# A decoder layer on one core: tile 5's search is held back in the recording until the search of tiles 7 and 6 is over

## The chip, the core and the metric

The kernel runs as one program on 1 core of a Trainium2 chip. The core has five engines with a queue of instructions each: TensorE (PE in the profile, with PEld for its weight loads), VectorE (DVE), ScalarE (ACT), GpSimd (POOL) and SyncE (SP, which issues the DMAs). Each queue is worked off in its order; an instruction that waits for another engine holds up all that stands behind it on its own engine. The metric is device time in microseconds for one execution of the whole layer.

## The reference, cut to what matters

The layer takes 1024 tokens of width 1024 and computes a mixer and a SwiGLU feed-forward part, each with a residual and a layer norm. The part around the change is the sparse attention of the mixer:

```python
logits = jnp.einsum('bqhd,bsd->bqhs', iqb, ik_f) * (IDX_DIM ** -0.5)      # 8 index heads
score = jnp.einsum('bqh,bqhs->bqs', w, jax.nn.relu(logits))
score = jnp.where(causal[None], score, -jnp.inf)
_, idx = lax.top_k(score, k_sel)                                          # 256 keys for each query
...
s = jnp.einsum('bqhd,bqkhd->bhqk', qb, kg) * (HEAD_DIM ** -0.5)
p = jax.nn.softmax(jnp.where(valid[:, None], s, -jnp.inf), axis=-1)       # 8 attention heads
o = jnp.einsum('bhqk,bqkhd->bqhd', p, vg)
```

Every query may look at the 256 keys with the highest score among those before it. Beside the attention the mixer has four groups of causal pooling on 512 channels (u), whose result goes through a small product (w_pool) into the output projection.

## The kernel before, in words

The 1024 queries are cut into 8 tiles of 128, on the partitions. Tile i sees 128(i+1) keys. Tiles 0 and 1 see at most 256 keys and need no selection; tiles 2 to 7 do. The stages that matter here come in this order:

1. **Score loop** (lines 788 to 818). For tiles 2 to 7, and for each of 8 index heads: TensorE makes `lg`, ScalarE its relu, VectorE adds it, weighted, onto `score_X` (8 VectorE instructions for each tile). GpSimd then writes the causal limit into the tile's last 128 columns.
2. **Projections** (to line 982). TensorE makes u, k and v (`pj` and `pair`). For each of the four pooling groups, VectorE's `ub_V<-ub_V` (u_split, line 856) is followed by ScalarE's copy `phi_V`, GpSimd's remainder `plo_V` and TensorE's `po`; GpSimd also makes the remainders of the weights (`ws_W`, w_split, line 906) for k and v. For each of 8 tiles of k, ScalarE and VectorE write the transposed keys (`kr_K`).
3. **Attention** (from line 982), in units of one head pair and one tile: four head pairs with tiles 7 and 6 in turn, then four with 5 and 4, then 3 and 2, then 1 and 0. A unit is: TensorE's `s`, VectorE's masking and maximum (an instruction that the profile calls CUSTOM_DVE_ANT_0, `sm_H<-s,score_X`, 128x1024 for tile 7, 128x768 for tile 5), ScalarE's exponential, GpSimd's normalization, TensorE's transposes `pT`, their copies by ScalarE and VectorE, and TensorE's product `o`.
4. Output projection, norm and feed-forward part, to the end.

The selection itself (`bisect`, line 642) is a binary search for the 256th value, in 31 steps on 16-bit halves of the score. One VectorE step is a comparison over all keys of a tile with an accumulated count (`junk_X<-keys...`) and two instructions on one number per query (`colsD_X` or `colsE_X`). After the last step come the masks: seven instructions that turn `score_X` into a mask of 0 and a large negative number. Four such searches exist. Tiles 4 and 3 share one and tile 2 has its own, both on ScalarE (`TILES_A`, columns `colsA_X`). Tiles 7 and 6 share one on VectorE (`colsD_X`, `keysD_T`), and tile 5 has its own on VectorE (`colsE_X`, `keys_T`, 128x768).

What sets the order. A search is a Python generator, called a stream here, which stops before each step and names the engine and the step's cost. While the other instructions are recorded, `fill` (line 768) is asked before each of them: it lets every stream advance whose next step fits, by the kernel's own table of costs, before that instruction's operands are ready. While the letters V, A and G are in `pinned` (from `open_stream`, line 745, to `pinned.clear()`, line 982) each instruction of VectorE, ScalarE and GpSimd is also marked to stay in the order in which it was recorded (line 175). Instructions recorded with the pins off carry no such mark: the framework's own scheduler places them on their engine among the others, as early as their data and its own estimate allow. A mask that isn't there yet when attention wants it is fetched by `need(i)` (line 764), called from `u_exp` (line 1041), which is after line 982, with the pins off: it advances tile i's stream until its mask is recorded.

Of the kernel before, what the change touches and what calls it, by code (L numbers as in the profile page):

```python
# [41 lines left out]
NORM = 2  # L42
NORM_SMALL = 2
STEP_ORDER = "SPNT"
COPY_N = 4
COPY_V = (0,)
START_A = 5
# [3 lines left out]
SLACK = {"V": 0.3, "A": 0.4}  # L51
# [130 lines left out]
def decoder_layer_kernel(  # L182
# [560 lines left out]
    streams = []  # L743
# [7 lines left out]
    def start(st):  # L751
        return max(st[0], queues[st[1][0]].t)

    def advance(st):
        fill, times.fill = times.fill, None
        q = queues[st[1][0]]
        try:
            st[1] = next(st[2])
        except StopIteration:
            streams.remove(st)  # L760
        st[0] = q.t
        times.fill = fill
# [4 lines left out]

    def fill(q, until):
        while True:
            todo = [st for st in streams if st[1][0] == q.name and start(st) + st[1][1] <= until + SLACK.get(q.name, 0.0)]  # L770
            if not todo:
                return
            advance(min(todo, key=lambda st: (start(st), -max(st[3]))))
# [293 lines left out]
    def u_trans(u):  # L1067
        g, pr, i = u
        for e, (sm, st) in enumerate(live.pop(u)[0]):
            for j0 in range(0, i + 1, 4):  # L1070
# [7 lines left out]
                n_cp[0] += 1  # L1078
                if n_cp[0] % COPY_N in COPY_V:
                    V.tensor_copy(dst, pv)  # L1080
# [53 lines left out]
    for n_, u in enumerate(units):  # L1134
        g, pr, i = u
        for step in STEP_ORDER:
            if step == "S":
# [398 lines left out]
    first = {}  # L1536
# [366 lines left out]
```

## Time and profile before

| | |
|---|---|
| median of 3 runs | 1336.13 us (1334.67 to 1336.29) |
| the profiled execution's own time | 1334.65 us |
| its span, first to last instruction | 1332.9 us |
| PE busy | 1201.6 us (90% of the span) |
| DVE busy | 1081.6 us (81%) |
| ACT busy | 640.0 us (48%) |
| POOL busy | 737.4 us (55%) |
| mean granted TensorE clock | 0.949 of full speed |

The shares are means over stages with different limits. In the strip of 40 slices of the page (33.3 us each, counted from 1) DVE reads 8 or 9 from slice 2 to slice 13, while PE falls to 6 in slices 11 and 12 and PEclk to 6 and 7 in slices 12 and 13: that is the end of the projections and the first part of attention. From slice 14 on the strip is led by PE.

### The profile page before, as it was taken

How to read it: one execution, taken by the hardware profiler on the slowest of the kernel's cores; microseconds unless marked ns; L12 is line 12 of the kernel's file. 1: busy time of each engine (PE TensorE's matmuls, PEld its weight loads, DVE VectorE, ACT ScalarE, POOL GpSimd, SP SyncE). 2: the span in 40 equal slices, each digit the busy share in tenths (PEclk: the TensorE clock that was granted, in tenths of full speed). 3: DMA queues.
4: the chain of work that ended last, by engine and by line, in shares of the span. 5: the costliest groups of instructions: out<-in, count | busy, mean ns of one | idle time of the engine just before them, and what ended most of it. 6: DMA issues, size and time to landing. Idle time of an engine off the chain costs nothing.

```text
span 1332.9 us, 16110 instructions
## 1 busy us (share of the span) xinstructions
PE 1201.6 (90%) x5462; PEld 936.7 (70%) x5462; DVE 1081.6 (81%) x1828; ACT 640.0 (48%) x1335; POOL 737.4 (55%) x509
## 2 busy tenths in 40 slices
PE   7979997888667997999789999999999999999996
PEld 6646575667434664788677878878787887878775
DVE  6898999999989788566687787777768787777698
ACT  3345785658756676535644343333333343333431
POOL 1392494565012354527678484755748485666848
PEclk8999998889867898999799999999999999999998
DMA  9540020302000066420030101112120101113113
GB/s 350 216 161 19 16 95 17 110 32 79 25 0 9 26 210 240 157 103 1 24 111 30 66 32 64 45 50 76 36 79 32 64 32 64 63 41 118 41 59 122
DMA packets 34904, 103.91 MB, mean 78 GB/s; under 512 B 3843, under 2 KB 3843, under 8 KB 33286
## 3 DMA queue, kind: packets, MB, share of 16 engines
q1 hardware_dynamic: 34822, 102.88, 21.6%
q8 instruction: 43, 0.70, 0.2%
q14 instruction: 39, 0.32, 0.1%
HBM read 93.42 MB, written 9.45 MB: 77 GB/s over the span
## 4 chain that ended last, share of the span: by engine, by line
PE 38%; DVE 6%; POOL 4%; issue 2%; ACT 1%; DVEq 0%; POOLq 0%; ACTq 0%
PE gu L169 24%; PE dn L169 14%; DVE act_W L169 2%; POOL wraw_R L169 1%; DVE utmp_X L169 1%; POOL wraw_W L169 1%; DVE gtmp_V L169 1%; POOL wblk_T L169 0%; DVE wblk_T L169 0%; DVE hr_H L169 0%; POOL hr_H L169 0%; DVE res_X L169 0%; DVE stat_C L169 0%; POOL wblk_V L169 0%; DVE wblk_V L169 0%
## 5 line engine op out<-in xcount | busy, mean ns | idle before, releaser
L169 PE MATMUL gu<-hr_H,wblk_T 128*128 128x512 f32 (+1 forms) x924 | 217.0, 387 | 2.9 <-POOL wblk_T L169 1.9
L169 PE MATMUL gu<-hr_H,wblk_V 128*128 128x512 f32 (+1 forms) x924 | 215.1, 384 | 3.7 <-POOL wblk_V L169 2.0
L169 PEld LDWEIGHTS gu<-hr_H,wblk_T 128*128 128x128 f32 x924 | 172.1, 191 | 39.0 <-POOL wblk_T L169 3.6
L169 PEld LDWEIGHTS gu<-hr_H,wblk_V 128*128 128x128 f32 x924 | 170.1, 188 | 40.1 <-POOL wblk_V L169 3.7
L169 DVE TENSOR_TENSOR res_X<-res_X,dn 128x512 f32<-128x512 f32 (+1 forms) x253 | 159.0, 678 | 15.2 <-PE dn L169 15.0
L169 POOL TENSOR_SCALAR sm_H<-sm_H,stat_X 128x1024 f32<-128x1024 f32 (+7 forms) x64 | 58.2, 922 | 152.7 <-DVE stat_X L169 109.9
L169 PE MATMUL pj<-ws_W,hT_H 128*128 128x512 f32 x456 | 120.2, 411 | 6.4 <-ACT pout_K L169 2.7
L169 POOL TENSOR_TENSOR wraw_R<-wraw_R 128x512 f32<-128x512 f32 x64 | 94.3, 1480 | 47.0 <-DVE wblk_T L169 23.7
L169 POOL TENSOR_TENSOR wraw_W<-wraw_W 128x512 f32<-128x512 f32 x60 | 86.6, 1450 | 58.0 <-DVE wblk_V L169 29.3
L169 PEld LDWEIGHTS pj<-ws_W,hT_H 128*128 128x128 f32 x456 | 85.9, 194 | 32.7 <-issue 11.5
L169 PE MATMUL dn<-wblk_T,act_W 128*128 128x512 f32 x324 | 79.8, 395 | 4.4 <-DVE act_W L169 4.4
L169 PE MATMUL dn<-wblk_V,act_W 128*128 128x512 f32 x324 | 78.5, 391 | 2.9 <-DVE act_W L169 2.5
L169 DVE TENSOR_SCALAR_CACHE_REDUCE junk_X<-keysD_T,colsD_X 128x1024 int16<-128x1024 int16 (+1 forms) x64 | 79.0, 1270 | 0.9
L169 PEld LDWEIGHTS dn<-wblk_T,act_W 128*128 128x128 f32 x324 | 61.0, 190 | 19.2 <-DVE act_W L169 6.5
L169 ACT ACTIVATE wblk_V<-wraw_R 128x512 fp32r<-128x512 f32 x56 | 35.3, 630 | 80.6 <-POOL wraw_R L169 62.2
L169 POOL TENSOR_TENSOR ws_W<-raw_R,ws_W 128x1024 fp32r<-128x1024 f32 x17 | 44.4, 2629 | 51.7 <-ACT ws_W L169 51.7
L169 PEld LDWEIGHTS dn<-wblk_V,act_W 128*128 128x128 f32 x324 | 60.4, 188 | 17.4 <-DVE act_W L169 4.2
L169 ACT ACTIVATE wblk_V<-wraw_W 128x512 fp32r<-128x512 f32 x53 | 33.1, 628 | 75.0 <-POOL wraw_W L169 56.4
L169 ACT ACTIVATE wblk_T<-wraw_W 128x512 fp32r<-128x512 f32 x56 | 35.0, 628 | 66.3 <-POOL wraw_W L169 50.2
L169 ACT ACTIVATE sm_H<-sm_H,stat_X 128x1024 f32<-128x1024 f32 (+7 forms) x64 | 49.0, 767 | 32.3 <-DVE stat_X L169 31.9
L169 ACT ACTIVATE wblk_T<-wraw_R 128x512 fp32r<-128x512 f32 x52 | 32.5, 627 | 60.9 <-POOL wraw_R L169 45.5
L169 PE MATMUL pT<-const_C,sm_H 128*128 128x128 f32 x288 | 48.3, 303 | 10.9 <-DVE qab_W L169 5.3
(305 smaller groups left out, 2812.2 us busy)
## 6 DMA issues: line engine op xcount, KB each, us to landing
wm_K<-in_wma_dram SPq DMA_DIRECT2D x16, 512.0 KB, 9.3
modraw_V<-in_wmc_dram SPq DMA_DIRECT2D x16, 512.0 KB, 4.5
wraw_R<-in_wg_dram SPq DMA_DIRECT2D x6, 1024.0 KB, 4.7
wraw_R<-in_wd_dram SPq DMA_DIRECT2D x12, 512.0 KB, 3.4
wraw_W<-in_wup_dram SPq DMA_DIRECT2D x12, 512.0 KB, 3.5
modraw_V<-in_wmg_dram SPq DMA_DIRECT2D x10, 512.0 KB, 4.3
wraw_R<-in_wup_dram SPq DMA_DIRECT2D x10, 512.0 KB, 3.5
wraw_W<-in_wg_dram SPq DMA_DIRECT2D x5, 1024.0 KB, 4.8
```

The lines of the kernel that those rows point to most:

```text
L169: ins_ = f(*a, **k)
```

## The change

`fill` no longer lets tile 5's stream advance as long as the stream of tiles 7 and 6 is open:

```diff
+LATE = [5]
...
     def fill(q, until):
         while True:
-            todo = [st for st in streams if st[1][0] == q.name and start(st) + st[1][1] <= until + SLACK.get(q.name, 0.0)]
+
+            first = [st for st in streams if 7 in st[3]]
+            todo = [st for st in streams if not (first and st[3] == LATE) and st[1][0] == q.name and start(st) + st[1][1] <= until + SLACK.get(q.name, 0.0)]
             if not todo:
                 return
             advance(min(todo, key=lambda st: (start(st), -max(st[3]))))
```

No instruction is added or taken away: each engine has the same instructions with the same operands. The stream of tiles 7 and 6 is still open when line 982 takes the pins off. So all of tile 5's steps and masks are now recorded without a mark, and the built program has them in other places on VectorE. The orders of GpSimd and SyncE are the same in both programs, and TensorE's is the same up to the attention of tiles 7 and 6. On ScalarE the steps of the two searches of tiles 4, 3 and 2 move a little.

VectorE at the end of the score loop, from the first score instruction of tile 7 (128x1024) to the first count of tiles 7 and 6 (`colsD_X<-score_X`). Before:

```order
L169 TENSOR_SCALAR score_X_77<-relu_K_563,const_C_78 128x1024
L169 SCALAR_TENSOR_TENSOR score_X_77<-relu_K_563,const_C_78,score_X_77 128x1024 x7
L169 TENSOR_SCALAR junk_X_607,colsD_X_615<-score_X_77 128x1024
L169 TENSOR_SCALAR junk_X_608,colsD_X_615<-score_X_77 128x896
L169 TENSOR_SCALAR colsD_X_615<-colsD_X_615 128x2 x3
```

The same place now, its last rows:

```order
L170 SCALAR_TENSOR_TENSOR score_X_77<-relu_K_563,const_C_78,score_X_77 128x1024
L170 SCALAR_TENSOR_TENSOR colsE_X_616<-colsE_X_616 128x1
L170 TENSOR_SCALAR junk_X_609,colsE_X_616<-keys_T_612,colsE_X_616 128x768
L170 SCALAR_TENSOR_TENSOR score_X_77<-relu_K_563,const_C_78,score_X_77 128x1024
L170 TENSOR_SCALAR colsE_X_616<-colsE_X_616 128x1
L170 SCALAR_TENSOR_TENSOR score_X_77<-relu_K_563,const_C_78,score_X_77 128x1024
L170 SCALAR_TENSOR_TENSOR colsE_X_616<-colsE_X_616 128x1
L170 TENSOR_SCALAR junk_X_609,colsE_X_616<-keys_T_612,colsE_X_616 128x768
L170 TENSOR_SCALAR junk_X_607,colsD_X_615<-score_X_77 128x1024
```

Tile 5's first count, its keys and five comparisons of its search now stand among the scores of tiles 6 and 7; before, none of them did.

VectorE around the third of the four pooling instructions `ub_V<-ub_V`. Before, with one step of tile 5 ahead of it (the third of 32 comparisons with `keys_T`):

```order
L169 SCALAR_TENSOR_TENSOR colsD_X_615<-colsD_X_615 128x2
L169 TENSOR_SCALAR junk_X_609,colsE_X_616<-keys_T_612,colsE_X_616 128x768
L169 TENSOR_SCALAR colsE_X_616<-colsE_X_616 128x1
L169 SCALAR_TENSOR_TENSOR colsE_X_616<-colsE_X_616 128x1
L169 SCALAR_TENSOR_TENSOR ub_V_1221<-ub_V_1221,ub_V_1222 128x1024
L169 TENSOR_SCALAR junk_X_607,colsD_X_615<-keysD_T_610,colsD_X_615 128x1024
```

The same place now, with the end of tile 5's search and its masks ahead of it:

```order
L170 TENSOR_SCALAR keys_T_612<-score_X_77,colsE_X_616 128x768
L170 TENSOR_SCALAR junk_X_609,colsE_X_616<-score_X_77,colsE_X_616 128x768
L170 TENSOR_SCALAR colsE_X_616<-colsE_X_616 128x1
L170 SCALAR_TENSOR_TENSOR score_X_77<-keys_T_612,colsE_X_616 128x768
L170 TENSOR_SCALAR score_X_77<-score_X_77 128x768
L170 TENSOR_TENSOR keys_T_612<-keys_T_612,score_X_77 128x768
L170 TENSOR_TENSOR junk_X_609<-junk_X_609,keys_T_612 128x768
L170 TENSOR_SCALAR score_X_77<-junk_X_609 128x768
L170 SCALAR_TENSOR_TENSOR ub_V_1221<-ub_V_1221,ub_V_1222 128x1024
L170 TENSOR_SCALAR junk_X_607,colsD_X_615<-keysD_T_610,colsD_X_615 128x1024
```

All 32 comparisons and all masks of tile 5 stand ahead of this instruction now, where 3 comparisons stood; ahead of the first `ub_V` it is 17 instead of 1, ahead of the second 29 instead of 2. Ahead of the first masking instruction of attention it is 32 instead of 20. From the first masking instruction of tile 5 on (128x768) the two orders hold the same work again.

## Rows read from the trace of the kernel before

**Rows 1.** Busy us by stretch: PE, PEld, DVE, ACT, POOL; then clock, DMA share, GB/s.
```profile
172.10:209.00 36.90, 33.75 (x148) 27.27 (x146) 36.06 (x62) 22.22 (x67) 27.70 (x19) 1.00 0.24 86
209.00:259.00 50.00, 39.05 (x135) 30.31 (x136) 48.85 (x78) 32.96 (x85) 28.34 (x16) 0.80 0.18 64
354.60:376.10 21.50, 2.61 (x7) 1.59 (x8) 20.11 (x49) 5.80 (x12) 0.00 (x0) 0.54 0.05 17
376.10:440.10 64.00, 50.76 (x224) 31.39 (x222) 56.25 (x135) 44.39 (x116) 16.35 (x14) 0.75 0.02 5
440.10:480.00 39.90, 37.06 (x251) 24.82 (x250) 32.13 (x75) 26.48 (x58) 14.55 (x14) 0.96 0.29 97
```

**Rows 2.** Waits of PE from 172 to 376 us: total us, times, longest.
```profile
PE s L169 <- DVE qab_H L169: 18.8, 1, 18.8
...
PE kT L169 <- DVE kr_K L169: 2.4, 1, 2.4
...
PE pj L169 <- DVE kr_K L169: 1.3, 1, 1.3
```

**Rows 3.** Busy DVE us of tile 5's `colsE_X` instructions by stretch; last row: all.
```profile
172.10:209.00 36.90, 2.72 (x10) 1.00 0.24 86
209.00:259.00 50.00, 2.83 (x9) 0.80 0.18 64
376.10:440.10 64.00, 21.36 (x58) 0.75 0.02 5
120.00:441.00 321.00, 52.74 (x145) 0.87 0.12 40
```

**Rows 4.** Timeline of DVE: start, us; two comparisons of tile 5 in a row.
```profile
361.75 1.07 DVE L169 TENSOR_SCALAR_CACHE_REDUCE junk_X<-keys_T,colsE_X 128x768 int16<-128x768 int16 x1
...
363.25 1.07 DVE L169 TENSOR_SCALAR_CACHE_REDUCE junk_X<-keys_T,colsE_X 128x768 int16<-128x768 int16 x1
```

**Rows 5.** Waits of DVE from 143.6 to 173 us.
```profile
DVE score_X L169 <- ACT relu_K L169: 1.8, 3, 0.8
DVE junk_X L169 <- POOL score_X L169: 1.5, 1, 1.5
```

**Rows 6.** Instructions on `colsE_X` and, for 209 to 250 us, `colsD_X`: ns min/median/max.
```profile
L169 DVE TENSOR_SCALAR colsE_X<-colsE_X x37: 132/153/155, 189.7 to 429.8; 128x1 f32<-128x1 f32 x35, 128x1 int16<-128x1 f32 x1, 128x1 int32<-128x1 int32 x1
L169 DVE SCALAR_TENSOR_TENSOR colsE_X<-colsE_X x31: 139/159/1214, 208.9 to 426.9; 128x1 f32<-128x1 f32 x31
...
L169 DVE SCALAR_TENSOR_TENSOR colsD_X<-colsD_X x6: 162/1808/2277, 213.8 to 243.7; 128x2 f32<-128x2 f32 x6
```

**Rows 7.** Timeline of DVE: third pooling instruction, and attention's first ones; tile 5's first.
```profile
238.81 1.23 DVE L169 SCALAR_TENSOR_TENSOR ub_V<-ub_V,ub_V 128x1024 f32<-128x1024 f32 x1
...
374.11 1.40 DVE L169 TENSOR_TENSOR qab_H<-qT,qab_H 64x512 fp32r<-64x512 f32 x2
376.10 1.22 DVE L169 CUSTOM_DVE_ANT_0 sm_H<-s,score_X 128x1024 f32<-128x1024 f32 x1 [0.58 <-PE s L169]
...
440.10 0.95 DVE L169 CUSTOM_DVE_ANT_0 sm_H<-s,score_X 128x768 f32<-128x768 f32 x1
```

**Rows 8.** Timeline of ACT and POOL behind the third pooling instruction.
```profile
240.06 1.06 ACT L169 ACTIVATE phi_V<-ub_V 128x1024 fp32r<-128x1024 f32 x1 [6.65 <-DVE ub_V L169]
...
241.20 2.39 POOL L169 TENSOR_TENSOR plo_V<-ub_V,phi_V 128x1024 fp32r<-128x1024 f32 x1 [3.71 <-DMA raw_R<-in_wv_dram]
243.56 4.69 POOL L169 TENSOR_TENSOR ws_W<-raw_R,ws_W 128x1024 fp32r<-128x1024 f32 x2
```

**Rows 9.** Timeline of PE: a product on those weights, then the last work before attention.
```profile
245.95 7.15 PE L169 MATMUL pair<-ws_W,hT_H 128*128 128x512 f32 x23 [2.56 <-POOL ws_W L169]
...
352.11 1.03 PE L169 MATMUL qT<-const_C,raw_R 128*128 128x128 f32 x8
354.64 1.35 PE L169 MATMUL s<-kr_K,qab_H 128*128 128x512 f32 x4 [1.49 <-ACT qab_H L169]
```

**Rows 10.** Timeline of ACT in attention: one comparison of tile 4's search.
```profile
388.39 0.81 ACT L169 ACTIVATE junkA_T<-keys_T,colsA_X 128x640 bf16<-128x640 uint16 x1
```

## The prediction, written before the changed kernel ran

> **What bounds the kernel now.** I read the busy time by stretch first, then tile 5's share of it, then who waits. From the end of the score loop (172.1 us) to the first masking instruction of tile 5 (440.1) VectorE is the busiest engine: 36.06 of 36.90 us, 48.85 of 50.00, and 20.11 of the 21.50 before attention begins, in which TensorE does 2.61 [rows 1]. TensorE's longest wait there is one of 18.8 us for VectorE's `qab_H` [rows 2]: it had the projections and the transposed queries of tile 7 ready at 352 us [rows 9], and attention's first masking instruction came at 376.1 [rows 7]. In the next 64.0 us VectorE is busy 56.25 us, 21.36 of them with tile 5's search [rows 1, 3]. So VectorE's queue sets the pace up to 440.1, TensorE's after it (37.06 of 39.90 us [rows 1]). What stands where in that queue is what the change alters.
>
> **What the change does.** By its words it holds tile 5 back. The order of the built program shows the opposite. Its steps are recorded after the pins are off, and the scheduler has put them ahead of work that they used to follow. All 32 comparisons and the masks stand before the third `ub_V`, where 3 comparisons stood, and before attention's first masking instruction, where 20 stood. No work is saved (52.74 us of tile 5 on VectorE in both [rows 3]). So three things count: the work that is pushed back, the wait that is filled, and what attention gains when tile 5 is out of its way.
>
> **1. VectorE reaches attention later.** Two comparisons of tile 5 in a row start 1.50 us apart [rows 4]. Twelve more of them stand ahead of attention now: 18.0 us. Its masks come too. What is left of the 21.36 us [rows 3] after twelve comparisons at the busy 1.07 of [rows 4] and their two small instructions at 0.15 and 0.16 (medians of [rows 6]), 16.6 us, is 4.8 us, to which I add 1.8 for the gaps and the few instructions between search and masks: 6.6. Together +24.6 us. Against it, in the score loop VectorE waited 1.8 us for ScalarE and 1.5 for GpSimd [rows 5], and tile 5's steps stand there now: -3.3.
>
> The third part is GpSimd. In a step, the instruction with two inputs on `colsE_X` has a median of 159 ns and a longest of 1214, while the one with a single input never took over 155; and between 209 and 250 us, where GpSimd works much, the same two-input instruction of tiles 7 and 6 has a median of 1808 [rows 6]. In the 21.50 us before attention GpSimd did nothing [rows 1], and a part of tile 5's search stood there; now it stands beside its work on `ws_W` and the pooling groups. Lower bound 0 (GpSimd has no more instructions than before, and each delays one VectorE instruction at most once). Upper bound: 24 steps move into that stretch (29 comparisons ahead of the second `ub_V`, less five in the score loop), each at 1.21 - 0.16 = 1.05: 25 us. I take +3, near the lower end, because in the trace the median of `colsE_X` is the short one although GpSimd worked beside its first steps. The Trainium skill, SBUF — State Buffer (Who interferes with whom), says that GpSimd and VectorE share a pair of ports as an exclusive lock and that a VectorE instruction with two SBUF inputs is held up whole by a reading GpSimd instruction. The trace agrees (159 ns against 1808). By it alone every moved step could be hit, and the sum would be the upper bound.
>
> VectorE: 24.6 - 3.3 + 3 = +24.3, so it is ready for attention at 376.1 + 24.3 = 400.4.
>
> **2. TensorE is late next.** The pooling chain runs through four queues in order: `ub_V` on VectorE, then `phi_V` on ScalarE (240.06, after a wait of 6.65 for it), `plo_V` on GpSimd, and behind `plo_V` in GpSimd's queue the weights `ws_W`, without which TensorE can't go on [rows 8, 9]. At the third `ub_V` (238.81 [rows 7]) tile 5 had used 2.72 + 2.83 = 5.55 us [rows 3] and will have used all 52.74: 47.2 us busy, or 51.3 at 1.50 us for each 1.38 busy. Less the 3.3 recovered, plus 3 for GpSimd: +51.0. TensorE resumes `pair` at 296.9 instead of 245.95. From there to the transposes of the queries (352.11 [rows 9]) its way is the same, without the waits of 2.4 and 1.3 us for `kr_K` [rows 2], since VectorE has less between those now; I add 1 us for the clock after the longer wait (it was 0.80 of full speed from 209 to 259 us, with waits [rows 1]). 352.1 + 51.0 - 3.7 + 1 = 400.4. From the transposes to the first masking instruction it takes 2.5 us to the first `s` [rows 9] and 2.0 from `qab_H` to the mask [rows 7]: 404.9. So TensorE takes over from VectorE as what is late, by 4 us, and attention starts **+28.8 us**. The 18.8 us that TensorE waited there are not gained. They turn into waits at `po` and `ws_W` earlier.
>
> Bounds: +21.3 (VectorE alone, GpSimd at its lower bound) and +50.8 (GpSimd at its upper bound, 22 us over the 3 taken).
>
> **3. The first half of attention gets shorter.** From the first mask of tile 7 to that of tile 5 (64.0 us) VectorE has 56.25 - 21.36 = 34.9 us left. ScalarE has 44.39, less three comparisons of tiles 4 and 3 that the order now has before attention, 3 x 0.81 [rows 10]: 42.0. TensorE has 50.76 at a clock of 0.75 [rows 1], 38.1 at full speed, and it comes to this stretch from work and not from a wait of 18.8 us. Three engines have about as much to do; none can fill the stretch. In the next one, led by TensorE, 37.06 x 0.96 = 35.6 us at full speed took 39.90, a share of 0.89. ScalarE's 42.0 at that share is 47.2. I take 47 us, so **-17**. Bounds: 42.0 (-22) with ScalarE never waiting, and 56 (-8) if TensorE starts cold again.
>
> From 440.1 on both programs have the same order on VectorE, so what is late there stays late: I see no work in it that could start before its units, and TensorE, which leads in the next stretch, waits there for the same units as before. I cost it at nothing.
>
> **Sum.** +28.8 - 17 = +11.8 us. The profiled execution took 1334.65 us, so 1346.5; the median of the runs is 1.5 us above it, which makes **1348 us**.
>
> **The rivals.** *A, not slower: VectorE alone counts.* If TensorE isn't late, attention starts at +21.3, and if ScalarE's work closes up to 42.0 us the stretch gives back 22.0: -0.7, or 1335 us. It decides wherever the stretch gets under 64.0 - 28.8 = 35 us with my start, or under 43 with VectorE's. For it speaks that VectorE was the busiest engine nearly throughout and that its work is the same. Against it: pooling and weights hang on `ub_V` one after the other, and TensorE is in front of attention by 18.8 us only, where it loses 51.
>
> *B, much slower: the start of attention costs more.* Place: the steps beside GpSimd, at about half the upper bound (+12 instead of +3), and a first half of attention of 52 us. Price: +37.8 - 12 = +26, or 1362 us. For it speaks the 1808 ns of tiles 7 and 6; against it the 155 ns limit of the single-input instruction, so that only one in three instructions of a step can be hit.
>
> *C, it does what it says:* tile 5's steps run after the masks of tiles 7 and 6. Then attention starts when TensorE is ready, at 352.1 + 4.5 = 356.6 or 19.5 us earlier, and all of tile 5, 52.74 us busy, stands beside the next stretch: 34.9 + 52.74 = 87.6 us instead of 64.0, +23.6. The sum is +4, or 1340 us. The order rules it out, as far as one engine's queue runs in its order.
>
> **Chances.** My forecast (+5 to +19) 0.60, A 0.15, B 0.22, C 0.03. A change of under 0.2% (2.7 us) can't be told from none with this kernel. A lies mostly within that, and partly below, and so a little of my forecast's lower side falls within it too: faster 0.08, same 0.11, slower 0.81. The range takes in A's upper half and B: 1336 to 1362 us; my forecast's own is 1341 to 1355.
>
> **What would show it.** In the changed kernel's trace: instructions on `colsE_X` from about 145 us and none after about 290; the third `ub_V` at about 290; TensorE idle for over 20 us before the first `po` and again before the second; no long wait for `qab_H`; the first mask of tile 7 at about 405 and of tile 5 at about 452. It is wrong in step 1 if VectorE passes the third `ub_V` far from 290, in step 2 if TensorE is found waiting for VectorE once more at `qab_H`, in step 3 if the stretch between the first masks of tiles 7 and 5 isn't 42 to 52 us, and altogether if that of tile 5 comes before 440.

## The result and the profile after

The changed kernel takes 1345.0 us (median of 3 runs, 1343.72 to 1346.84) against 1336.13: a ratio of 1.0071 with a 95% interval of 1.0048 to 1.0094. It is slower, by 8.9 us, and 1348 had been forecast. The profiled execution took 1345.0 us with a span of 1343.2, 10.3 more than the span before.

I cut both profiles at 172 us (the end of the score loop before; in the changed kernel the first count of tiles 7 and 6 comes at 176.86) and at three events of the program: the first masking instruction of tile 7, that of tile 5 and that of tile 3. First busy us by stretch of the kernel before; columns as in [rows 1].

```profile
110.00:172.00 62.00, 57.52 (x259) 38.05 (x258) 53.24 (x65) 42.75 (x71) 24.66 (x18) 1.00 0.04 14
172.00:376.10 204.10, 160.62 (x655) 127.16 (x655) 198.10 (x366) 134.21 (x366) 101.31 (x65) 0.88 0.17 58
376.10:440.10 64.00, 50.76 (x224) 31.39 (x222) 56.25 (x135) 44.39 (x116) 16.35 (x14) 0.75 0.02 5
440.10:490.81 50.71, 47.18 (x319) 31.91 (x318) 40.98 (x96) 35.89 (x78) 19.60 (x18) 0.97 0.37 122
```

The same of the changed kernel:

```profile
110.00:172.00 62.00, 57.03 (x256) 37.41 (x255) 57.23 (x83) 42.14 (x69) 22.22 (x16) 1.00 0.04 15
172.00:395.56 223.56, 164.78 (x659) 129.43 (x658) 211.44 (x410) 135.23 (x377) 100.85 (x65) 0.85 0.16 53
395.56:450.50 54.94, 48.17 (x216) 29.00 (x215) 36.43 (x72) 42.05 (x105) 15.50 (x14) 0.76 0.02 6
450.50:499.84 49.34, 47.10 (x329) 31.71 (x327) 40.71 (x96) 37.36 (x81) 19.77 (x18) 1.00 0.38 127
```

Attention starts 19.5 us later, its first half (mask of tile 7 to mask of tile 5) is 9.1 us shorter, and the rest is nearly the same: it is 10.4 us late at tile 5, 9.0 at tile 3 and 10.3 at the end. The third number behind the comma is VectorE's busy time; length less busy is called its waiting here, the short gaps between instructions included. Up to tile 3's first mask VectorE is busy 348.6 us before and 345.8 after, so it has no more to do; it waits 32.2 us before and 44.0 after. Of these 11.8 us more, 10.8 lie in the first half of attention (7.8 to 18.5) and 6.1 ahead of it; 4.0 were won up to 172 us and 1.1 behind the first half. Most of what is new ahead of attention are waits at the keys:

```profile
DVE kr_K L170 <- ACT kr_K L170: 5.2, 5, 1.8
```

VectorE's timeline, in answer to [rows 7]:

```profile
275.23 1.22 DVE L170 SCALAR_TENSOR_TENSOR ub_V<-ub_V,ub_V 128x1024 f32<-128x1024 f32 x1
...
393.57 1.41 DVE L170 TENSOR_TENSOR qab_H<-qT,qab_H 64x512 fp32r<-64x512 f32 x2 [1.24 <-ACT qab_H L170]
395.56 1.23 DVE L170 CUSTOM_DVE_ANT_0 sm_H<-s,score_X 128x1024 f32<-128x1024 f32 x1 [0.58 <-PE s L170]
...
436.30 1.23 DVE L170 CUSTOM_DVE_ANT_0 sm_H<-s,score_X 128x1024 f32<-128x1024 f32 x1 [3.91 <-PE s L170]
...
445.89 1.09 DVE L170 CUSTOM_DVE_ANT_0 sm_H<-s,score_X 128x896 f32<-128x896 f32 x1 [5.12 <-PE s L170]
```

TensorE's waits from 172 to 410 us, in answer to [rows 2] (total us, times, longest), and then its timeline ahead of attention, in answer to [rows 9]:

```profile
PE pair L170 <- POOL ws_W L170: 16.5, 4, 5.0
PE po L170 <- ACT ub_V L170: 14.9, 1, 14.9
PE po L170 <- ACT phi_V L170: 11.3, 1, 11.3
PE pair L170 <- ACT ws_W L170: 7.3, 1, 7.3
...
PE s L170 <- ACT qab_H L170: 1.7, 1, 1.7
```

```profile
390.21 1.03 PE L170 MATMUL qT<-const_C,raw_R 128*128 128x128 f32 x8
392.97 3.28 PE L170 MATMUL s<-kr_K,qab_H 128*128 128x512 f32 x8 [1.73 <-ACT qab_H L170]
```

The wait of 18.8 us for `qab_H` is gone; those on the pooling chain (`po` and `ws_W`) have grown from 16.8 to 52.0 us. TensorE reaches the transposes of the queries 38.1 us later, and now VectorE waits for what comes from it: at the keys and at `qab_H` behind ScalarE's part, and twice for long inside the first half.

### The profile page after: what moved, and what is told of

Same layout as the page of the kernel before. It is cut to its first block, busy times and chain, and to the rows that moved or that the text cites. A ratio compares the mean times of both kernels' runs of the same rounds, so it can differ in the third digit from the quotient of the medians.

```text
span 1343.2 us, 16107 instructions
## 1 busy us (share of the span) xinstructions
PE 1200.3 (89%) x5462; PEld 933.6 (70%) x5462; DVE 1077.9 (80%) x1828; ACT 639.9 (48%) x1335; POOL 734.5 (55%) x509
## 4 chain that ended last, share of the span: by engine, by line
PE 37%; DVE 6%; POOL 4%; issue 2%; ACT 1%; DVEq 0%; POOLq 0%; ACTq 0%
PE gu L170 23%; PE dn L170 14%; DVE act_W L170 2%; POOL wraw_R L170 1%; DVE utmp_X L170 1%; POOL wraw_W L170 1%; DVE gtmp_V L170 1%; POOL wblk_T L170 0%; DVE wblk_T L170 0%; DVE hr_H L170 0%; POOL hr_H L170 0%; DVE res_X L170 0%; DVE stat_C L170 0%; POOL wblk_V L170 0%; DVE wblk_V L170 0%
## 5 line engine op out<-in xcount | busy, mean ns | idle before, releaser
L170 PE MATMUL pj<-ws_W,hT_H 128*128 128x512 f32 x456 | 117.5, 404 | 3.9 <-DVE const_C L170 1.7
L170 PEld LDWEIGHTS pj<-ws_W,hT_H 128*128 128x128 f32 x456 | 83.8, 190 | 29.4 <-issue 10.1
L170 PE MATMUL pair<-ws_W,hT_H 128*128 128x512 f32 x144 | 44.1, 468 | 19.3 <-POOL ws_W L170 12.0
## 6 DMA issues: line engine op xcount, KB each, us to landing
wm_K<-in_wma_dram SPq DMA_DIRECT2D x16, 512.0 KB, 10.1
```

The source lines that it names most:

```text
L170: ins_ = f(*a, **k)
```

## The experiments

All times are medians; each ratio is to runs of the kernel before on the same chip. "Mask 7", "5" and "3" are the starts of the first masking instructions of these tiles in the profiled execution, busy and waiting are VectorE's from 110 us to mask 3, as above. From mask 3 to the end each program takes 842 to 847 us, so most of what a change does is settled there. The profiled execution lies up to 4.4 us off its kernel's median (e5: 1331.8 against 1327.3), so positions and medians agree no better than that.

| run | us | ratio to before, 95% | mask 7 | mask 5 | mask 3 | busy | waiting |
|---|---|---|---|---|---|---|---|
| before | 1336.13 | | 376.1 | 440.1 | 490.8 | 348.6 | 32.2 |
| changed | 1345.0 | 1.0071 [1.0048, 1.0094] | 395.6 | 450.5 | 499.8 | 345.8 | 44.0 |
| e1_held | 1339.6 | 1.0016 [1.0003, 1.0030] | 355.3 | 452.9 | 497.1 | 347.4 | 39.7 |
| e2_half | 1349.5 | 1.0102 [1.0087, 1.0117] | 372.1 | 459.1 | 503.8 | 345.8 | 48.0 |
| e3_chain | 1346.6 | 1.0085 [1.0070, 1.0101] | 409.1 | 459.4 | 505.2 | 354.5 | 40.8 |
| e4_warm | 1341.1 | 1.0040 [1.0025, 1.0055] | 395.1 | 448.0 | 497.3 | 345.1 | 42.2 |
| e5_split20 | 1327.3 | 0.9931 [0.9912, 0.9950] | 372.9 | 437.1 | 482.7 | 340.7 | 32.0 |
| e6_split10 | 1328.5 | 0.9944 [0.9928, 0.9959] | 362.9 | 442.6 | 483.5 | 342.8 | 30.6 |
| e7_split20_warm | 1326.4 | 0.9926 [0.9909, 0.9942] | 372.3 | 435.7 | 480.7 | 341.3 | 29.4 |
| e8_chain_off | 1336.7 | 1.0004 [0.9994, 1.0013] | 395.9 | 444.3 | 489.7 | 337.7 | 42.0 |
| e9_cols_split | 1332.8 | 0.9964 [0.9950, 0.9977] | 380.3 | 436.4 | 485.7 | 327.9 | 47.8 |
| e10_cols_split_before | 1318.8 | 0.9863 [0.9846, 0.9880] | 355.2 | 430.5 | 472.8 | 329.0 | 33.8 |
| e11_best | 1313.8 | 0.9825 [0.9808, 0.9841] | 359.9 | 423.9 | 467.4 | 320.9 | 36.5 |

**e1: tile 5 really held back.** In `advance`, VectorE is pinned while a step of tile 5 is recorded:

```
+        own = st[3] == LATE and "V" not in pinned
+        if own:
+            pinned.add("V")
         ...
+        if own:
+            pinned.discard("V")
```

> The changed kernel, with VectorE's queue kept in written order also while tile 5's steps are recorded in attention, so that none of its 32 comparisons can be moved ahead: by the order all 32 stand behind attention's first masking instruction. Theory 1 (the loss of 9 us comes from work of tile 5 that stands ahead of the pooling chain and of attention): the third ub_V is back near 235 us, attention starts when TensorE is ready, first mask of tile 7 at 354 to 360 us, no 18.8 us wait for qab_H; the first mask of tile 5 at about 445 because VectorE has 35 + 53 = 88 us of work up to it; in all 1336 to 1344 us, faster than the changed kernel. Theory 2 (holding tile 5 back costs by itself, wherever its steps land): 1345 us or more.

Most of the loss is gone, attention starts at 355.3 us and the third `ub_V` is at 236.3. So what cost the changed kernel its time is the work that was moved ahead, as theory 1 says. But nothing is gained over before either: tile 5's block now ends in front of its first unit, and TensorE stands still for it. Tile 5's first mask came at 452.9 us, where 445 had been expected: VectorE's work of 88.96 us fills most of the first half (its row, then TensorE's timeline at the end of it):

```profile
355.32:452.91 97.59, 62.12 (x322) 40.77 (x322) 88.96 (x242) 51.70 (x122) 17.04 (x16) 0.75 0.02 6
```

```profile
453.93 2.50 PE L170 MATMUL s<-kr_K,qab_W 128*128 128x512 f32 x6 [21.48 <-DVE stat_X L170]
```

**e2: 20 comparisons ahead, 12 and the masks in written order.** As e1, with `own` true only from the 24th step on.

> The changed kernel, but only the first 20 comparisons of tile 5 may be moved ahead; the other 12 and the masks are kept in written order in attention. Ahead of attention stand then as many comparisons as before the change (20), but 17 more of them than before ahead of the third ub_V. So VectorE's amount is that of before and only the pooling chain is late. Theory 1 (chain and amount count separately, the chain by about 1.25 us for each comparison): third ub_V at about 260 us instead of 238.8, TensorE at the queries' transposes at about 374 instead of 352, its wait for qab_H under 3 us, first mask of tile 7 at 376 to 380; total within 4 us of before, 1333 to 1340. Theory 2 (TensorE's lateness is what costs, VectorE's amount doesn't): most of the loss remains, 1342 us or more.

A miss. The third `ub_V` came at 252.6 us, `qab_H` was waited for 1.7 us, and attention started at 372.1, earlier than before, all as theory 1 has it or better; but the median is the highest of all (its interval overlaps those of e3 and of the changed kernel). TensorE's longest wait from 372 us on is of 14.1 us, for VectorE at tile 5's first unit:

```profile
PE s L171 <- DVE stat_X L171: 18.6, 8, 14.1
```

The order has all 12 comparisons and the masks between the 16th and the 17th masking instruction, so VectorE waited 20 us earlier in that half and then made TensorE wait. Theory 2's number came true, by another mechanism; e5 takes that mechanism away.

**e3: the same amount ahead, behind the pooling chain.** The planner's filling leaves tile 5 out; its steps start behind the fourth `ub_V`, three at each projection group:

```
+        for _ in range(PACE * (n_ > 9)):
+            for st in streams:
+                if st[3] == LATE:
+                    advance(st)
```

> The changed kernel with none of tile 5's steps ahead of the fourth ub_V; from there on its steps are recorded in order, three at each projection group, so that all 32 comparisons and the masks stand ahead of attention as in the changed kernel, but the pooling chain is not delayed. Theory 1 (VectorE's amount ahead of attention costs by itself): third ub_V near 235 us, TensorE waits again, at the projections and over 15 us at qab_H, first mask of tile 7 at 395 to 402 us, total 1342 to 1352. Theory 2 (only the late chain costs): first mask of tile 7 before 382 us, and with a first half of attention of 55 us a total of 1320 to 1332.

The third `ub_V` was early (233.9 us) and the loss stayed; the work ahead of attention costs by itself, since VectorE is busy for 226.7 of the 237.1 us from 172 to the first mask. TensorE waits not at `qab_H`, as expected (1.5 us), but at the keys that VectorE writes late:

```profile
PE kT L171 <- DVE kr_K L171: 37.7, 3, 29.6
PE pj L171 <- DVE kr_K L171: 17.9, 2, 10.5
```

Mask 7 came later than theory 1 said (409.1 for 395 to 402): VectorE's busy time is 8.6 us more than in the changed kernel, and this is the only order in which it lies above that of before.

**e4: TensorE busy in its short wait.**

```
+            warm = psA("warm")
+            for _ in range(FILLER):
+                tc.keep_in_program_order(T.transpose(warm[:, 0:P], ident, ident))
```

> The changed kernel with 14 transposes of the identity (nobody reads them) behind the transposes of the queries, so that TensorE has work in its wait of 1.73 us for qab_H. In the changed kernel the granted clock is 1.00 up to 390 us and 0.50 from 395.5 to 410, and VectorE waits 14 us for s up to tile 5's first mask. Theory 1 (the slow clock behind that short wait is the reason why the first half of attention took 54.9 us and not 47): the clock stays at 1.00, the stretch between the first masks of tiles 7 and 5 becomes 48 to 52 us, total 3 to 7 us less. Theory 2 (the clock falls because of the waits between the s units, or TensorE isn't what sets the pace there): the stretch stays at 54 to 56 us and the total within 1.5 us of the changed kernel's.

The changed kernel from 390 to 405 us, then the run with the transposes:

```profile
390.00:395.00 5.00, 3.27 (x16) 2.01 (x14) 3.67 (x6) 4.90 (x10) 0.00 (x0) 0.92 0.31 105
395.00:400.00 5.00, 3.85 (x9) 2.00 (x8) 4.38 (x7) 4.95 (x9) 0.00 (x0) 0.50 0.01 2
400.00:405.00 5.00, 5.00 (x10) 2.00 (x8) 2.58 (x6) 5.00 (x15) 1.95 (x2) 0.50 0.00 0
```

```profile
390.00:395.00 5.00, 4.81 (x30) 3.35 (x28) 3.70 (x7) 4.90 (x10) 0.00 (x0) 1.00 0.32 105
395.00:400.00 5.00, 3.22 (x9) 1.40 (x8) 4.77 (x8) 4.95 (x10) 0.00 (x0) 0.73 0.01 2
400.00:405.00 5.00, 5.00 (x10) 2.43 (x10) 2.41 (x5) 5.00 (x15) 2.21 (x2) 0.50 0.00 0
```

The granted clock held out a few us longer and then fell to its lower level (0.50, which is 1.2 GHz) all the same. The first half took 52.9 us instead of 54.9, between the two theories. The total is 3.9 us less; all four runs lie below the three of the changed kernel (1340.6 to 1342.3 against 1343.7 to 1346.8), but the intervals of the two ratios still touch, so some gain is likely and its size is not shown.

**e5 and e6: how much goes ahead.** The first steps of tile 5 are recorded ahead of the queries' split and are free to move; the next step is pinned behind it; the rest is free again and spreads over the first half (e5 `HOIST = 23`, 20 comparisons; e6 `HOIST = 13`, 10).

```
+    need(7)
+    need(6)
+    st5 = next(st for st in streams if st[3] == LATE)
+    for k_ in range(HOIST):
+        advance(st5)
     for i in (7, 6):
         q_make(i, qr[i], qp[i])
+    pinned.add("V")
+    advance(st5)
+    pinned.discard("V")
```

> The changed kernel, with the first 20 comparisons of tile 5 free to move ahead (they stand ahead of the second ub_V, as in the run with 20 before it) and one step behind them tied to the queries' split of attention, so that the other 12 comparisons and the masks can't pass it but are spread freely over the first half of attention, as before the change. Ahead of attention VectorE has what it had before the change; only the pooling chain is late. Theory 1 (the run with 20 was slow only because its 12 comparisons and masks stood in written order in one block ahead of tile 5's first unit, with TensorE waiting 14 us for it; the late chain costs nothing as long as TensorE reaches the queries before VectorE): first mask of tile 7 at 371 to 374 us, first mask of tile 5 at 434 to 441, total 1331 to 1338. Theory 2 (the late chain itself costs): 1342 or more.

> As the run before, with 10 comparisons of tile 5 free to move ahead instead of 20, and 22 and the masks spread over the first half of attention. Theory 1 (what counts is how long VectorE waits in all up to about 490 us, since its busy time there is the same in every order): ahead of attention it waits less, as the chain is hardly late (third ub_V at 240 to 245), first mask of tile 7 at 358 to 362; in the first half it has 71 us of work and waits under 10, so the first mask of tile 5 comes at 432 to 441 and the total is 1328 to 1338. Theory 2 (comparisons in attention stand in the way of TensorE's units, as in the run that held all of them back): 1339 or more.

Both are faster than before, by 0.7 and 0.6%. Theory 2 fails in both; theory 1 has e6's total right and its range for e5 was too high. But its reason, that VectorE's busy time is the same in every order, doesn't hold: of the 8.2 and 7.4 us that the two are ahead of before at mask 3, 7.9 and 5.8 lie in the busy time (348.6 to 340.7 and 342.8) and the rest in waiting. Why these orders keep VectorE busy for less, no run separates. In e5 the third `ub_V` is at 253.7 us, 14.8 later than before, and TensorE reaches the queries at 368.1; that lateness costs nothing, since it takes only from the 18.8 us that TensorE used to wait. Its stretches up to mask 5:

```profile
172.00:372.92 200.92, 159.95 (x662) 126.61 (x660) 190.35 (x351) 135.24 (x376) 100.97 (x65) 0.90 0.18 59
372.92:437.08 64.16, 54.54 (x236) 32.71 (x238) 58.73 (x146) 46.26 (x113) 16.73 (x14) 0.76 0.03 9
```

Against the changed kernel: the last 12 comparisons and the masks go back into the first half of attention, which grows by 9.2 us, while its start comes 22.6 us earlier. VectorE waits 5.4 us in that half instead of 18.5.

**e7: e5 with idle transposes**, 14 as in e4 and 5 behind the scores of each of the first four units.

> The run with 20 comparisons ahead and 12 spread, with transposes of the identity that nobody reads: 14 behind the queries' transposes and 5 behind the scores of each of attention's first four units. Theory 1 (gaps of about half a microsecond between the first units are what keeps the granted clock at 0.50 for the first 15 us): clock over 0.8 in the 15 us from the first s on, total 3 to 6 us under the run without them. Theory 2 (VectorE sets the pace in that stretch, since it has 56 us of work in 64): within 2 us of the run without them.

Theory 2: within 1 us of e5, and the clock was at 0.50 from 380 to 390 us in both.

**e8: the pooling chain off VectorE.** `u_split` does on GpSimd what wrote `ub_V` on VectorE; the planner's account is kept as it was.

```
-        V.scalar_tensor_tensor(cur[:, 16:PADW], cur[:, 16:PADW], 1.0 / WINDOWS[g], own[:, 16:PADW], ALU.mult, ALU.subtract)
+        G.tensor_scalar(cur[:, 16:PADW], cur[:, 16:PADW], 1.0 / WINDOWS[g], None, ALU.mult)
+        G.tensor_tensor(cur[:, 16:PADW], cur[:, 16:PADW], own[:, 16:PADW], ALU.subtract)
```

> The changed kernel, with the pooling difference that writes ub_V taken from VectorE to GpSimd, as a scaling and a subtraction (no other work is changed, and tile 5's 32 comparisons still stand ahead of the projections' end). The pooling chain no longer passes VectorE's queue. Theory 1 (VectorE's queue is what makes TensorE late at po and ws_W): the waits of 14.9 and 11.3 us at po are gone, TensorE reaches the queries' transposes before 365 us and waits over 10 us for qab_H; attention starts when VectorE is ready, 380 to 390 us; total 1331 to 1341. Theory 2 (GpSimd becomes the late one, with 4 x 3.5 us more in its queue ahead of ws_W): TensorE waits for ws_W over 25 us in all, total 1343 or more.

The waits at `po` are down to about 2 us each, as expected, and the total lies in theory 1's range, but not on its way: TensorE then waits at the next thing from VectorE's queue, and attention starts where it did.

```profile
325.54 1.09 PE L170 MATMUL kT<-const_C,rope_V 128*128 128x128 f32 x4 [43.55 <-DVE kr_K L170]
```

Of the 10.1 us won on the changed kernel up to mask 3, 8.1 lie in VectorE's busy time, and 4.9 of these are the four `ub_V` that GpSimd took over. Why the first half is 48.3 us there, with the clock at 0.86 in place of 0.76, no run separates; what differs is named under step 3 below.

**e9 and e10: the form of the small instructions**, in the changed kernel and in the one before.

```
-                V.tensor_scalar(pr, cntc, 0.0, float(1 << b), ALU.is_ge, ALU.mult)
+                for m in range(nt):
+                    V.tensor_scalar(one(pr, m), one(cntc, m), 0.0, float(1 << b), ALU.is_ge, ALU.mult)
...
-                V.scalar_tensor_tensor(cand, pr, off, cand, ALU.add, ALU.add)
+                for m in range(nt):
+                    V.tensor_scalar(one(cand, m), one(pr, m), off, one(cand, m), ALU.add, ALU.add)
```

> The changed kernel, with the two small instructions of every search step on VectorE written as instructions of one column and one tensor input each (four for tiles 7 and 6, two for tile 5) instead of two instructions, one of them with two tensor inputs. The arithmetic is the same. In every trace so far the one-input instruction on one column of tile 5 never took over 0.155 us, while those on two columns (median 0.17) and those with two inputs took up to 2.4 us where GpSimd works. Theory 1 (the form of the instruction decides whether GpSimd can hold it up, so the held-up time of about 25 us is what these forms cost): the small instructions stay under 0.2 us, VectorE's busy time up to tile 3's first mask falls from 346 to 325 to 335 us in spite of 9 us more for the added instructions, total 8 to 18 us less than the changed kernel's. Theory 2 (GpSimd's held-up time moves to other VectorE instructions, so that it is conserved): busy time rises to 350 to 356 and the total is 2 to 9 us more.

> The kernel before the change with the same four or two small instructions of one column and one input in every search step of VectorE; the planner then puts 16 comparisons of tile 5 ahead of attention instead of 20. Theory 1 (the form decides): total 1318 to 1330. Theory 2 (the held-up time moves on): 1336 to 1345.

Theory 1 in both: VectorE's busy time falls by 17.9 and 19.6 us, the total by 12.2 and 17.3 (by the ratios 14 and 18). The instructions of the two searches on `colsD_X` and `colsE_X`, the added ones included, take 20.0 and 23.6 us less up to mask 3 (188.6 to 168.6, 190.2 to 166.6). The order moved as well, 16 comparisons ahead instead of 20 in e10, and e5 shows that an order alone can be worth 7.9 us of busy time; so the form has most of the gain, and its exact share is not shown. In the changed kernel a part of it turns into waiting (44.0 to 47.8), since TensorE is late there; before the change less does.

**e11: e7 with the small instructions of e9.**

> The run with 20 comparisons ahead, 12 spread and TensorE's idle transposes, with the small instructions of one column and one input as well. If both gains add (9.7 us for the split, 8 to 18 for the form): 1308 to 1320. If the form gives nothing: 1326 to 1334. If VectorE's shorter queue only makes it wait for TensorE, whose way to the queries' transposes is set by the late ub_V: 1320 to 1327.

The result is 1313.8 us, 1.75% (1.59 to 1.92) under before and the best of all. It lies in the range for two gains that add: e7 was 0.7% under before, and e9 1.1% under the changed kernel.

## Why the prediction was right, and where its terms were off

**What the change does.** Right, and e1 confirms it: the loss hangs on the steps that moved ahead. What the change says, e1 builds; rival C had priced it at 1340, and it took 1339.6. Its parts fit less well than its sum: the start at 355.3 us agrees with 356.6, but the first half took 97.6 us where 87.6 had been set, and 6.5 came back up to mask 3. The 52.74 us of tile 5 "in both" became 55.03 (below).

**Step 1, VectorE later: too large.** Without the 6.1 us that VectorE newly waits ahead of attention it would have been ready 13.3 us later, not 24.3. Two terms failed. The 1.50 us from one comparison to the next is a pace with gaps; among other instructions the moved steps brought almost none (from 172 us to the third `ub_V` VectorE is busy 65.28 of 66.81 us before and 101.15 of 103.23 after). And GpSimd's term was +3 for the moved steps alone: these did cost 2.3 us more, but the steps of tiles 7 and 6, which I had left out, gave back 5.5. VectorE's busy time from 172 us to the third `ub_V` on `colsE_X` and on `colsD_X`, before and then after:

```profile
172.00:238.81 66.81, 5.48 (x18) 0.88 0.18 65
...
172.00:238.81 66.81, 54.30 (x74) 0.88 0.18 65
```

```profile
110.00:172.00 62.00, 7.84 (x18) 1.00 0.04 15
172.00:275.23 103.23, 47.19 (x128) 0.80 0.16 50
...
172.00:275.23 103.23, 48.81 (x74) 0.80 0.16 50
```

Tile 5 adds 41.7 us, and the same 74 instructions of tiles 7 and 6 take 5.5 us less. Another 7.84 us of tile 5 had been done up to 172 us, so all of it takes 55.03 us where it took 52.74.

**Step 2, TensorE late next: right in kind, 9.3 us too large.** The third `ub_V` is 36.4 us late where I had 51.0. Of the 14.6 us, 6.2 are GpSimd's term (+3 forecast, 2.3 - 5.5 measured), some 4 the gaps, and some 4.5 the score loop (7.84 us of tile 5 done there, where 3.3 had been taken off). Against that, TensorE did not make up 2.7 us from there to the queries but lost 1.7, and 0.9 more up to the mask. Its waits at the first two late `po` were 14.9 and 11.3 us, and not over 20 each. Start of attention: +19.5, just under my lower bound of +21.3.

**Step 3, the shorter first half: 9.1 us and not 17.** By the sign that I had named, 42 to 52 us, this step is wrong: it took 54.9. I had TensorE arrive warm, because it comes from work. It did come from work, at a clock of 1.00 up to 390 us, and had 0.50 from 395 to 410. So the size is near the other bound that I had named for a cold start, -8. VectorE, rid of tile 5, waited 14.2 us for `s`:

```profile
DVE sm_H L170 <- PE s L170: 14.2, 7, 5.1
```

The slow start is only a part of it. Of these 14.2 us, 9.0 lie at 436.30 and 445.89. Ahead of them TensorE had stood for VectorE, which wrote tile 3's masks until 429.7 us and `ws_W` behind them, and the clock had fallen a second time:

```profile
430.15 1.64 PE L170 MATMUL pT<-const_C,sm_H 128*128 128x128 f32 x10 [2.56 <-DVE ws_W L170]
```

```profile
350.00:390.00 40.00, 40.00 (x178) 32.21 (x177) 36.32 (x68) 38.87 (x128) 5.68 (x5) 1.00 0.10 34
395.00:410.00 15.00, 13.85 (x37) 8.30 (x36) 8.59 (x17) 14.01 (x32) 4.22 (x4) 0.50 0.00 1
410.00:430.00 20.00, 16.30 (x92) 9.84 (x90) 18.65 (x38) 13.19 (x35) 7.04 (x6) 0.97 0.00 1
430.00:440.00 10.00, 9.31 (x33) 5.30 (x35) 5.32 (x11) 8.14 (x21) 2.01 (x2) 0.59 0.09 26
```

The same wait for `ws_W` (2.6 to 2.9 us) stands in e4 and e9, whose first halves took 52.9 and 56.2 us; in e3 and e8 it is 0.3 us or nothing, and these took 50.3 and 48.3. No run takes this wait away by itself, so how the 7.9 us divide between the two falls stays open.

**Sum.** 19.5 - 9.1 = +10.4 against +11.8: the two misses, 9.3 and 7.9 us, nearly cancel. The direction and the path were right; that the total came within 3 us is luck. Behind mask 5 nothing came of the rest, as costed.

**Rivals.** A (VectorE alone counts) fails in the kernel as built, as TensorE is late there and the first half did not close up to 42.0 us; its start of +21.3 is nearer to +19.5 than mine, but by a term for VectorE that was too large. B's mechanism, hold-ups by GpSimd on the moved steps of +12 us, was 2.3 in the changed kernel; e3 shows the nearest to it, with tile 5's instructions at 58.2 us and busy time 5.9 us over before.

What I did not see is which work belongs where. Rid of tile 5, the first half of attention still takes 48 to 56 us (the changed kernel, e3, e4, e8, e9), though VectorE has 36 to 39 us of work in it. Tile 5's last 12 comparisons and masks, 21 us, lengthen it by 9 when they are spread there (e5); they cost their length ahead of it (the change) and more in one block (e2).

## What to carry to other kernels

Cut two profiles at the same events and add up, for the engine with the most work, busy and waiting up to each. The change left the busy part nearly as it was (348.6 and 345.8 us) and paid in waits; e5, e6 and e7 won most of theirs in the busy part. So neither half may be taken as fixed by the order. In these runs the moved work cost least in small pieces, in a stretch that another engine paces; before moving instructions "later" in the source, look at what the scheduler does with those that are no longer pinned. And look at the maximum beside the median of tiny instructions: here a change of their form (e10) was worth about twice what the whole reordering cost.

## What the runs showed of the hardware

Whether GpSimd's work holds one of VectorE's small search instructions up goes by the instruction's form. That it is GpSimd shows in the ends: before, 26 of the 162 TENSOR_SCALAR and SCALAR_TENSOR_TENSOR on `colsA_X`, `colsD_X` and `colsE_X` alone took over 400 ns, and each of them ended within 31 ns of the end of a GpSimd instruction. Two of them, each behind the GpSimd instruction with which it ends:

```profile
211.38 2.35 POOL L169 TENSOR_TENSOR plo_V<-ub_V,phi_V 128x1024 fp32r<-128x1024 f32 x1 [10.87 <-ACT phi_V L169]
212.63 1.12 DVE L169 TENSOR_SCALAR colsD_X<-colsD_X 128x2 f32<-128x2 f32 x1
213.69 1.89 POOL L169 TENSOR_TENSOR ub_V<-ub_V 128x1024 f32<-128x1024 f32 x1
213.79 1.81 DVE L169 SCALAR_TENSOR_TENSOR colsD_X<-colsD_X 128x2 f32<-128x2 f32 x1
```

Small instructions on `colsD_X` between 209 and 250 us (ns min/median/max), before (its two-input one is in [rows 6]) and in e10:

```profile
L169 DVE TENSOR_SCALAR colsD_X<-colsD_X x7: 169/1191/2029, 212.6 to 248.5; 128x2 f32<-128x2 f32 x7
```

```profile
L169 DVE TENSOR_SCALAR colsD_X<-colsD_X x37: 142/170/209, 208.9 to 240.3; 128x1 f32<-128x1 f32 x36, 128x2 int32<-128x2 int32 x1
```

The instruction with one input was held up too, on two columns, and on one column it is not; my step 1 had only the two-input form in view. The held-up time did not move on to other instructions: it is gone from VectorE's busy time (348.6 to 329.0 us). The Trainium skill, SBUF — State Buffer (Who interferes with whom), adds to its rule on two inputs that a one-input instruction in a mode with two ports contends as well. The Trainium skill, VectorE: DVE Perf Modes (Mode 2×_2P — use both read ports for one tensor), says that such a mode wants the outermost dimension that is not one to be even, or odd and equal in source and destination. The trace agrees for two columns (1191 ns); a single column has no such dimension, and here it was not held up (170 ns).

TensorE's granted clock went from 1.00 (2.4 GHz) to 0.50 (1.2 GHz) behind a wait of 1.73 us and came back only at about 410 us, though TensorE had been at work without a pause from 350 to 390 (rows of step 3; e4's rows show the fall). It fell again behind the wait of 2.56 us that ended at 430.15. Filling the first wait, and those behind the first units (e7), put the fall off by a few us and did not prevent it.
